# Hybrid encoder trunk on one core: attention steps queued ahead of waiting steps, the delta net's end cut into three steps, a residual's root ahead of a product

## The chip, the cores and the metric

The kernel runs on one core of a Trainium2 chip. TensorE (PE) multiplies matrices, VectorE (DVE), ScalarE (ACT) and GpSimd (POOL) do the rest, SyncE (SP) issues most of the transfers. Each engine works through its own queue in order, and semaphores tie the queues together. The metric is device time in microseconds (us), the median of several executions.

## The reference

Two layers over 256 tokens of width 2048. Each layer has a token mixer of three head groups on one input projection, and then a dense SwiGLU block; each of the two ends in a normed residual.

```python
def hybrid_layer(x, ...):
    h = rmsnorm(x, pre_mix_norm)
    proj = h @ w_in
    c_q, c_kv, conv_in, g_q, g_k, g_v, g_z, a_f, b_f, a_b, b_b = jnp.split(proj, ...)
    o_a = mla_mixer(c_q, c_kv, ...)          # attention, 8 heads
    o_b = conformer_conv(conv_in, ...)       # depthwise convolution, width 31
    o_c = gdn_mixer(g_q, g_k, g_v, g_z, ...) # delta net, 4 heads, both directions
    mix = jnp.concatenate([o_a, o_b, o_c], axis=-1) @ w_out
    x = x + rmsnorm(mix, post_mix_norm)
    h = rmsnorm(x, pre_ffn_norm)
    f = (jax.nn.silu(h @ w_gate) * (h @ w_up)) @ w_down
    return x + rmsnorm(f, post_ffn_norm)
```

All is float32. The end of the delta net is `rmsnorm(o_f + o_b, out_norm) * silu(z)`.

## The kernel before

A float32 product is made of three products: each operand is split into a high half and a remainder (`hilo`, lines 328 and 329), and L353, L354 and L355 multiply high by high, remainder by high and high by remainder. `dense` takes the weights in units of two blocks of 128 rows: one transfer of 512 KB into `ws`, the split into `wh` (ACT, L328) and `wl` (DVE, L329), then twelve products of 128x512 on PE. There are five buffers each of `ws`, `wh` and `wl`, so the split may run up to five units ahead of the products.

After each unit, `dense` calls `bg.step(BUDGET)`. The object `bg` holds the background tasks in a list: generators that issue a few instructions and yield a cost. A step takes tasks from the front of the list and lets each advance once, until the costs have used up the budget of 1.6. A negative yield sends a task to sleep for as many units. `add(..., first=True)` puts a task in front of the list, otherwise it goes to the end. `ensure(name)` runs a task to its end at once, with no product of `dense` in between.

The tasks of a mixer are, in short: `gdn` (the delta net: `gdn_prep`, then `gdn_mats` for four heads, then four `gdn_head` that advance together, then the end, L892 to L918), `att0` to `att3` (`attend`, two attention heads each) and `conf` (the convolution; it alone may advance more than once in a unit). What `gdn` does in order:

- In `gdn_mats` each head ends in two sums, the second of which is L736 on DVE; after the fourth head the 16x16 blocks go to DRAM and come back in another layout (tiles `cd` and `Mt`), and DVE inverts them row by row (L753, L755).
- `gdn_head` doubles the inverses in three levels (PE L795, L802, L806; DVE L797, L808, L810) and applies them in five stages, each one set of products on PE and then work on DVE or ACT: L819 and L821, L826 and L827 (ACT), L832, L833 and L837, L840 (ACT), L846 and L849, L857 and L860. Four heads follow one another in every stage.
- The end squares and sums the outputs (ACT L898, DVE L899), forms a reciprocal root of 8 columns in fourteen dependent small operations on DVE, scales twice (L909, L910) and transposes on PE (L914).

`attend` rotates the queries on DVE (`rotate`, L538 to L541, then the remainder L999), transposes the rotated half on PE (L1012), forms the scores (L1022 to L1026), the softmax (DVE L1028 to L1039, ACT L1033), transposes it (L1044) and multiplies by the values (L1051).

The mixer's output projection runs in two passes over the four blocks of columns: pass one takes the eight blocks of rows that belong to attention, pass two starts with the four of the delta net. Ahead of the first products of pass two stands `ensure("gdn")`. In the last block of columns of a residual's product, `ev` squares the result on ACT (L1204), weighs it on DVE (L1205), and calls `residual`, which forms the reciprocal root (L257 to L270) and adds to `xs` (L495).

The order in which instructions are written is changed once more when the program is put together: a scheduler lays each engine's queue out, so that the queue's order, not the text's, tells what stands ahead of what.

Of the kernel before, what the change touches and what calls it, by code (L numbers as in the profile page):

```python
# [13 lines left out]
ALU = mybir.AluOpType  # L14
# [39 lines left out]
def kernel(  # L54
# [8 lines left out]
    act, dve, pe, pool, sync = nc.scalar, nc.vector, nc.tensor, nc.gpsimd, nc.sync  # L63
# [9 lines left out]
    def U(dt=F32):  # L73
        return upool.tile([P, 512], dt, tag="u", name="u")

    def TP(dt=F32):
        return psb.tile([P, 512], dt, tag="tp", name="tp")

    def SM(n, tag=None):
        return small.tile([P, n], F32, tag=tag or f"sm{n}", name="sm")  # L80

    def v3(ap, a):
        return ap.rearrange("p (a b) -> p a b", a=a)
# [16 lines left out]
    first = const.tile([P, P], F32, name="first")  # L100
# [8 lines left out]
    ps = TP()  # L109
# [126 lines left out]
    def rsqrt(v, mul, eps, n, tag):  # L236

        w = SM(n, f"rsw{n}")
        y = SM(n, tag + "y")
        t = SM(n, f"rst{n}")  # L240
        dve.tensor_scalar(out=w, in0=v, scalar1=mul, scalar2=eps, op0=ALU.mult, op1=ALU.add)
        dve.tensor_scalar(out=y.bitcast(I32), in0=w.bitcast(I32), scalar1=1, scalar2=None,
                          op0=ALU.logical_shift_right)
        dve.tensor_scalar(out=y.bitcast(I32), in0=y.bitcast(I32), scalar1=-1,
                          scalar2=0x5F3759DF, op0=ALU.mult, op1=ALU.add)
        for _ in range(3):
            dve.tensor_tensor(out=t, in0=y, in1=y, op=ALU.mult)
            dve.scalar_tensor_tensor(out=t, in0=t, scalar=-0.5, in1=w, op0=ALU.mult, op1=ALU.mult)
            dve.scalar_tensor_tensor(out=y, in0=t, scalar=1.5, in1=y, op0=ALU.add, op1=ALU.mult)
        return y  # L250

    def rsqrt_sum(v, part, mul, eps, tag):

        pre = SM(1, tag + "p")
        dve.tensor_reduce(out=pre, in_=v, axis=AX.X, op=ALU.add)  # L257
        dve.tensor_scalar(out=pre, in0=pre, scalar1=eps / mul, scalar2=None, op0=ALU.add)
        w = SM(3, tag + "w")
        z = SM(1, tag + "z")  # L260
        a = SM(1, tag + "a")
        dve.tensor_scalar(out=w[:, 0:1], in0=part, scalar1=pre[:, 0:1], scalar2=64.0 * mul,
                          op0=ALU.add, op1=ALU.mult)
        dve.tensor_scalar(out=z.bitcast(I32), in0=w[:, 0:1].bitcast(I32), scalar1=-0.5,
                          scalar2=float(0x5F3759DF - 2 ** 31), op0=ALU.mult, op1=ALU.add)
        for i in range(1, 3):
            dve.tensor_scalar(out=w[:, i:i + 1], in0=w[:, 0:1], scalar1=4.0 ** -i, scalar2=None, op0=ALU.mult)
        for i in range(3):
            dve.scalar_tensor_tensor(out=a, in0=z, scalar=w[:, i:i + 1], in1=z, op0=ALU.mult, op1=ALU.mult)
            dve.scalar_tensor_tensor(out=z, in0=a, scalar=-3.0, in1=z, op0=ALU.add, op1=ALU.mult)  # L270
        return z
# [48 lines left out]
    bg = Background()  # L320
# [166 lines left out]
            dve.tensor_reduce(out=ssq[:, t:t + 1], in_=part, axis=AX.X, op=ALU.add)  # L487
        return rsqrt(ssq, 1.0 / DM, EPS, NT, name)

    def residual(t, parts, ssqp, rname):  # L490

        r = rsqrt_sum(ssqp[t][:, 0:3], ssqp[t][:, 3:4], 1.0 / DM, EPS, rname)
        for c in range(4):
            xv = xs[:, t, c * 512:(c + 1) * 512]
            ins = dve.scalar_tensor_tensor(out=xv, in0=parts[(c, t)], scalar=r[:, 0:1], in1=xv,  # L495
                                           op0=ALU.mult, op1=ALU.add)
        if t == 0:
            hold[:] = [(1, ins)]
# [9 lines left out]
    for l in range(DEPTH):  # L508
# [357 lines left out]
        def together(*gens):  # L866

            live = list(gens)
            while live:
                cost = rest = 0.0  # L870
                for g in list(live):
                    try:
                        c = next(g) or 0.0
                        rest = max(rest, -c)
                        cost += max(c, 0.0)
                    except StopIteration:
                        live.remove(g)
                yield -rest if rest > 0 else cost

        def gdn():  # L880
            bg.ensure("sq", "sk", "sv")
            while not G:
                yield -1
            yield from gdn_prep()
            yield from gdn_mats()
            if PAIRS:
                yield from together(gdn_head(0), gdn_head(1))
                yield from together(gdn_head(2), gdn_head(3))
            else:
                yield from together(*[gdn_head(h) for h in range(GH)])  # L890

            while not gz:  # L892
                yield -1
            rq = G["rn"][:, 0:8]
            ossq = SM(8, "ossq")
            for t in range(NT):
                sq = U()
                act.activation(out=sq, in_=osb[t], func=AF.Square)  # L898
                dve.tensor_reduce(out=ossq[:, t * 4:t * 4 + 4], in_=v3(sq, 4), axis=AX.X, op=ALU.add)  # L899
                yield 0.7  # L900
            rq2 = SM(8, "rq2")
            dve.tensor_tensor(out=rq2, in0=rq, in1=rq, op=ALU.mult)
            dve.tensor_tensor(out=ossq, in0=ossq, in1=rq2, op=ALU.mult)
            ro = rsqrt(ossq, 1.0 / (128.0 * 128.0), EPS, 8, "ro")
            dve.tensor_scalar(out=rq2, in0=rq, scalar1=128.0 ** -0.5, scalar2=None, op0=ALU.mult)
            dve.tensor_tensor(out=ro, in0=ro, in1=rq2, op=ALU.mult)
            yield 1.2
            for t in range(NT):
                dve.tensor_tensor(out=v3(osb[t], 4), in0=v3(osb[t], 4), in1=bc(ro[:, t * 4:t * 4 + 4], 2, P), op=ALU.mult)  # L909
                dve.tensor_tensor(out=osb[t], in0=osb[t], in1=gz[t], op=ALU.mult)  # L910
                yield 1.3
                ps = TP()
                for h in range(GH):
                    pe.transpose(ps[:, h * P:(h + 1) * P], osb[t][:, h * P:(h + 1) * P], ident)  # L914
                hi, lo = U(F32R), U(F32R)
                hilo_col(hi, lo, ps, vcol(l, ONORM, 0))
                ocT.append((hi, lo))
                yield 0.7  # L918


        obT = []
# [206 lines left out]
        def pair(hp):  # L1128
            qn = [U(), U()]
            kv = [U(), U()]  # L1130

            def ev_q(t, ps):
                act.activation(out=qn[t][:, 0:384], in_=ps, func=AF.Identity, scale=lq["r"][:, t:t + 1])

            def ev_kv(t, ps):
                act.activation(out=kv[t], in_=ps, func=AF.Identity, scale=lkv["r"][:, t:t + 1])
            bg.ensure("lq")
            dense(pair_lhs(lq["T"]), list(range(4)), 384, wload(w_uq[l], 384 * hp, 384), ev_q)
            bg.ensure("lkv")
            dense(pair_lhs(lkv["T"]), list(range(4)), 512, wload(w_ukv[l], 512 * hp, 512), ev_kv)  # L1140
            bg.ensure("rope_k")
            bg.add(f"att{hp}", attend(hp, qn, kv))

        for n, step in enumerate(ORDER.split()):
            kw = dict(pre=lambda: rxb.append(row_rstd(l, "rx")), head=HEADG, mid=mid_mix) if n == 0 else {}
# [14 lines left out]
            elif step == "ckv":  # L1160
                o, ssq = latent_kv()
# [15 lines left out]
        wpm = post_weight(post_mix_norm, l)  # L1177
# [8 lines left out]
        def out_proj(lhs, passes, w, wpm, rname, need, after0):  # L1186
            parts = {}
            ssqp = [SM(4, "ssqp0"), SM(4, "ssqp1")]
            for i, ks in enumerate(passes):
                last = i == len(passes) - 1  # L1190
                for nb in range(4):
                    if i == 0:
                        parts[(nb, 0)], parts[(nb, 1)] = U(), U()

                    def ev(t, ps):
                        o = parts[(nb, t)]
                        if not last:
                            act.copy(out=o, in_=ps)
                            return
                        if i > 0:  # L1200
                            dve.tensor_tensor(out=o, in0=o, in1=ps, op=ALU.add)
                            ps = o
                        junk = U()
                        act.activation(out=junk, in_=ps, func=AF.Square, accum_out=ssqp[t][:, nb:nb + 1])  # L1204
                        dve.tensor_tensor(out=o, in0=ps, in1=wpm[nb], op=ALU.mult)  # L1205
                        if nb == 3:
                            residual(t, parts, ssqp, rname)
                    dense(lhs, ks, 512, wload(w, nb * 512, 512), ev, need=need,
                          **(dict(tail=TAILG, after0=after0) if last and nb == 3 else {}))

# [250 lines left out]
```

## Time and profile before

| | |
|---|---|
| median of 3 runs | 2233.1 us (2231.53 to 2233.45) |
| the profiled execution | 2234.73 us, of which the span of the core's instructions is 2233.0 us |
| PE busy | 2203.0 us, 99% of the span, mean granted clock 0.998 |
| DVE busy | 1762.0 us, 79% of the span |
| ACT busy | 1182.5 us, 53% of the span |

"Busy" is the time in which an instruction of the engine was under way. PE is at work nearly all the time, so the time can change by the microseconds in which PE waits, or runs at half its clock. The granted clock is the share of 2.4 GHz that PE was given: 1.00 is 2.4 GHz, 0.50 would be 1.2 GHz.

### The profile page before, as it was taken

The page shows a single profiled execution, that of the slowest core. Times are in us where ns is not written, and L with a number is a line of the kernel's source. Part 1 is how long each engine was busy: PE and PEld are TensorE (multiplying, and loading weights), DVE is VectorE, ACT ScalarE, POOL GpSimd, SP SyncE. Part 2 cuts the span into 40 slices and gives each one's busy share as a digit, 9 for nine tenths or more (in the row PEclk, how much of TensorE's full clock was granted, in tenths as well). Part 3 has the DMA queues.
Part 4 walks back from the last instruction along what each step waited for, and adds up shares of the span by engine and source line. Part 5 has one row for each costly group of instructions (what it writes and reads, how often), then busy time and mean ns, then how long its engine had stood idle before and what let it go on. Part 6 is the DMA issues. An engine that isn't in the chain of part 4 may idle for free.

```text
span 2233.0 us, 29215 instructions
## 1 busy us (share of the span) xinstructions
PE 2203.0 (99%) x10483; PEld 1839.3 (82%) x10483; DVE 1762.0 (79%) x2873; ACT 1182.5 (53%) x1642; POOL 45.9 (2%) x93
## 2 busy tenths in 40 slices
PE   8999999999999999999999999999999999999998
PEld 7988887788888888888879888877888888888886
DVE  6777998899999897544486779979999998975444
ACT  6665545555555555444356655455555555554432
POOL 2000000000000000000000000000000000000000
PEclk9999999999999999999999999999999999999999
DMA  7554525546656656555556545245565566665553
GB/s 254 171 178 146 188 89 162 162 164 207 217 181 217 225 189 223 171 195 192 179 172 186 183 142 171 97 153 161 188 207 208 191 215 214 202 214 178 191 196 124
DMA packets 218545, 407.75 MB, mean 183 GB/s; under 512 B 17607, under 2 KB 30065, under 8 KB 218400
## 3 DMA queue, kind: packets, MB, share of 16 engines
q1 hardware_dynamic: 215360, 397.72, 54.3%
q0 software_dynamic: 3008, 8.16, 1.3%
q8 instruction: 82, 1.34, 0.2%
q14 instruction: 63, 0.52, 0.1%
q10 hardware_dynamic: 32, 0.01, 0.0%
HBM read 402.94 MB, written 2.90 MB: 182 GB/s over the span
## 4 chain that ended last, share of the span: by engine, by line
PE 92%; DVE 5%; DMA 1%; issue 0%; ACT 0%; SPq 0%; DVEq 0%; ACTq 0%; POOLq 0%
PE acc L1306 19%; PE tp L1306 19%; PE acc L353 16%; PE acc L354 16%; PE acc L355 16%; DVE wl L329 1%; DVE xs L495 1%; PE tp L1230 1%; PE tp L1051 1%; DVE u L950 1%; DMA cd<-u 1%; PE tp L795 0%; PE tp L802 0%; PE tp L1022 0%; DMA xs<-in_x_dram 0%
## 5 line engine op out<-in xcount | busy, mean ns | idle before, releaser
L328 ACT CAST wh<-ws 128x1024 fp32r<-128x1024 f32 (+3 forms) x820 | 815.5, 1010 | 795.2 <-PE acc L354 409.6
L329 DVE TENSOR_TENSOR wl<-ws,wh 128x1024 fp32r<-128x1024 f32 (+3 forms) x820 | 942.1, 1170 | 336.2 <-ACT wh L328 332.2
L353 PE MATMUL acc<-wh,u 128*128 128x512 f32 (+2 forms) x1792 | 695.5, 389 | 0.4
L354 PE MATMUL acc<-wh,u 128*128 128x512 f32 (+2 forms) x1792 | 686.2, 383 | 3.5 <-DVE u L329 1.8
L355 PE MATMUL acc<-wl,u 128*128 128x512 f32 (+2 forms) x1792 | 685.6, 383 | 3.0 <-DVE wl L329 3.0
L354 PEld LDWEIGHTS acc<-wh,u 128*128 128x128 f32 x1792 | 337.5, 188 | 68.4 <-DVE u L333 4.1
L355 PEld LDWEIGHTS acc<-wl,u 128*128 128x128 f32 x1792 | 336.8, 188 | 68.1 <-DVE wl L329 5.8
L353 PEld LDWEIGHTS acc<-wh,u 128*128 128x128 f32 x1792 | 337.3, 188 | 62.3 <-ACT u L332 2.5
L1306 PE MATMUL acc<-wh,u 128*128 128x512 f32 x1220 | 376.4, 389 | 0.0
L1306 PE MATMUL tp<-wh,u 128*128 128x512 f32 x1220 | 375.8, 389 | 0.0
L1306 PEld LDWEIGHTS acc<-wh,u 128*128 128x128 f32 x1220 | 228.7, 188 | 47.9 <-DVE u L329 0.6
L1306 PEld LDWEIGHTS tp<-wh,u 128*128 128x128 f32 x1220 | 228.9, 188 | 47.6
L1306 PE MATMUL acc<-wl,u 128*128 128x512 f32 x610 | 237.4, 389 | 0.0
L1306 PE MATMUL tp<-wl,u 128*128 128x512 f32 x610 | 237.3, 389 | 0.0
L1306 PEld LDWEIGHTS acc<-wl,u 128*128 128x128 f32 x610 | 114.5, 188 | 23.7
L1306 PEld LDWEIGHTS tp<-wl,u 128*128 128x128 f32 x610 | 114.5, 188 | 23.7
L950 DVE SCALAR_TENSOR_TENSOR u<-u,cols 128x241 f32<-128x241 f32 (+14 forms) x240 | 101.0, 470 | 0.0
L1344 ACT CAST wh<-ws 128x1024 fp32r<-128x1024 f32 x60 | 63.0, 1050 | 28.4 <-PE tp L1306 12.8
L1345 DVE TENSOR_TENSOR wl<-ws,wh 128x512 fp32r<-128x512 f32 x60 | 41.1, 686 | 23.8 <-ACT wh L1344 21.8
L328 ACT CAST u<-u 128x512 fp32r<-128x512 f32 (+2 forms) x48 | 27.8, 587 | 38.2 <-DVE u L448 34.2
L1329 ACT ACTIVATE u<-u,sm 128x512 f32<-128x512 f32 x40 | 28.8, 724 | 34.6 <-DVE u L1376 24.4
L1351 DVE TENSOR_TENSOR ws<-ws 128x512 f32<-128x512 f32 x60 | 41.5, 692 | 2.0
(303 smaller groups left out, 1541.8 us busy)
## 6 DMA issues: line engine op xcount, KB each, us to landing
ws<-in_w_gate_dram SPq DMA_DIRECT2D x176, 512.0 KB, 5.0
ws<-in_w_up_dram SPq DMA_DIRECT2D x176, 512.0 KB, 4.8
ws<-in_w_down_dram SPq DMA_DIRECT2D x176, 512.0 KB, 3.6
ws<-in_w_in_dram SPq DMA_DIRECT2D x112, 512.0 KB, 4.3
ws<-in_w_out_dram SPq DMA_DIRECT2D x64, 512.0 KB, 3.7
ws<-in_w_ukv_dram SPq DMA_DIRECT2D x16, 512.0 KB, 3.7
ws<-in_w_uq_dram SPq DMA_DIRECT2D x16, 384.0 KB, 3.5
ws<-in_w_in_dram SPq DMA_DIRECT2D x10, 444.0 KB, 4.1
```

Of the source, the lines that this page charges most:

```text
L328: act.copy(out=hi, in_=src)
L329: dve.tensor_tensor(out=lo, in0=src, in1=hi.bitcast(F32), op=ALU.subtract)
L353: pe.matmul(o, xh, rh, start=(i == 0), stop=False)
L354: pe.matmul(o, xl, rh, start=False, stop=False)
L355: pe.matmul(o, xh, rl, start=False, stop=(i == len(ks) - 1))
L495: ins = dve.scalar_tensor_tensor(out=xv, in0=parts[(c, t)], scalar=r[:, 0:1], in1=xv, op0=ALU.mult, op1=ALU.add)
L950: dve.scalar_tensor_tensor(out=o, in0=i, scalar=wc, in1=o, op0=ALU.mult, op1=ALU.add)
L1306: pe.matmul(o, a, b, start=count[i] == 1, stop=count[i] == total[i])
L1329: act.activation(out=sg[t], in_=x, func=AF.Silu, scale=rfb[0][:, t:t + 1])
L1344: act.copy(out=wh, in_=wg)
L1345: dve.tensor_tensor(out=wl[:, 0:512], in0=b11, in1=wh[:, 0:512].bitcast(F32), op=ALU.subtract)
L1351: dve.tensor_tensor(out=b21, in0=b21, in1=b22, op=ALU.subtract)
```

## The change

Three edits. Attention tasks are put in front of the list of background tasks instead of at its end. The end of the delta net yields three times (2.6, 2.0, 2.0) where it yielded seven times (0.7, 0.7, 1.2, 1.3, 0.7, 1.3, 0.7). In the last block of columns of a residual's product the weighing is written after the reciprocal root, not ahead of it. No instruction is added or taken away on PE, DVE, POOL or SP.

```diff
-    def residual(t, parts, ssqp, rname):
+    def residual(t, parts, ssqp, rname, weigh):
         r = rsqrt_sum(ssqp[t][:, 0:3], ssqp[t][:, 3:4], 1.0 / DM, EPS, rname)
+        weigh()
         for c in range(4):
...
                 dve.tensor_reduce(out=ossq[:, t * 4:t * 4 + 4], in_=v3(sq, 4), axis=AX.X, op=ALU.add)
-                yield 0.7
...
             dve.tensor_tensor(out=ro, in0=ro, in1=rq2, op=ALU.mult)
-            yield 1.2
+            yield 2.6
             for t in range(NT):
...
                 dve.tensor_tensor(out=osb[t], in0=osb[t], in1=gz[t], op=ALU.mult)
-                yield 1.3
                 ps = TP()
...
                 ocT.append((hi, lo))
-                yield 0.7
+                yield 2.0
...
             bg.ensure("rope_k")
-            bg.add(f"att{hp}", attend(hp, qn, kv))
+            bg.add(f"att{hp}", attend(hp, qn, kv), first=True)
...
-                        dve.tensor_tensor(out=o, in0=ps, in1=wpm[nb], op=ALU.mult)
+
+                        def weigh():
+                            dve.tensor_tensor(out=o, in0=ps, in1=wpm[nb], op=ALU.mult)
                         if nb == 3:
-                            residual(t, parts, ssqp, rname)
+                            residual(t, parts, ssqp, rname, weigh)
+                        else:
+                            weigh()
```

The change moves work along the queues at three places. Line numbers of the changed kernel differ by one or two from those before; the prediction uses the numbers of before.

**PE, the last stages of the delta net's heads.** Before, as queued, with products of `dense` (L353 to L355) between the stages:

```order
L826 MATMUL tp<-u 128x128 x8
L353 MATMUL acc<-wh,u 128x512
L354 MATMUL acc<-wh,u 128x512
L355 MATMUL acc<-wl,u 128x512
...
L832 MATMUL tp<-u 128x128
L833 MATMUL tp<-u 128x128
...
L846 MATMUL tp<-u 128x128 x8
...
L857 MATMUL tp<-u 128x128 x16
...
L914 MATMUL tp<-ident,u 128x128 x8
```

Between L826 and L832 stand twelve products of `dense`, as many between L833 and L846 and between L846 and L857, and 72 between L857 and the transposes L914. In the change the same stages (each line number one higher, L914 now L913) stand so:

```order
L827 MATMUL tp<-u 128x128 x8
L833 MATMUL tp<-u 128x128
L834 MATMUL tp<-u 128x128
...
L847 MATMUL tp<-u 128x128 x8
L858 MATMUL tp<-u 128x128 x16
L913 MATMUL tp<-ident,u 128x128 x8
L353 MATMUL acc<-wh,u 128x512
L956 MATMUL tp<-ident,u 128x128 x2
L354 MATMUL acc<-wh,u 128x512
```

What moved: the heads advance later, so that `ensure("gdn")` finds their last stages and the whole end still to do, and issues them in one piece; between L827 and L913 no product of `dense` is left.

**DVE, around the wait for the 16x16 blocks.** Before, the remainder of the rotated queries of the second attention task (L999) stands ahead of the first instruction that reads the blocks (L753):

```order
L736 TENSOR_REDUCE u<-tp 128x32
L329 TENSOR_TENSOR wl<-ws,wh 128x1024
L329 TENSOR_TENSOR u<-tp,u 128x256 x2
L538 TENSOR_TENSOR u<-u,tab 128x128
...
L329 TENSOR_TENSOR wl<-ws,wh 128x768
L999 TENSOR_TENSOR u<-u 128x4x64
L753 TENSOR_TENSOR u<-u 128x1
```

In the change the last sum over a head (now L737) comes after both evacuations of the convolution's gated input (L1124, before L1125), and the rotation for the third attention task (L539 to L542, L998) comes behind the first eight rows of the inversion (L754, L756):

```order
L1124 SCALAR_TENSOR_TENSOR u<-acc,sm,u 128x512 x2
L737 TENSOR_REDUCE u<-tp 128x32
L329 TENSOR_TENSOR wl<-ws,wh 128x768 x2
L946 TENSOR_SCALAR u<-u,cols 128x256 x4
L949 SCALAR_TENSOR_TENSOR u<-u,cols 128x241 x4
L949 SCALAR_TENSOR_TENSOR u<-u,cols 128x242 x2
L754 TENSOR_TENSOR u<-u 128x1
...
L539 TENSOR_TENSOR u<-u,tab 128x128
...
L329 TENSOR_TENSOR wl<-ws,wh 128x1024
L998 TENSOR_TENSOR u<-u 128x4x64
```

From L754 up to and with L998 there stand eight rows of the inversion (sixteen instructions), four of the convolution (L949), four splits of weights, eight instructions of the rotation and L998.

**DVE, the last residual of the program.** Before, the weighing (L1205) stands ahead of the root:

```order
L1205 TENSOR_TENSOR u<-acc,u 128x512
L262 TENSOR_SCALAR sm<-sm 128x1
L264 TENSOR_SCALAR sm<-sm 128x1
L267 TENSOR_SCALAR sm<-sm 128x1 x2
L269 SCALAR_TENSOR_TENSOR sm<-sm 128x1
```

In the change it stands behind the root's first instruction:

```order
L262 TENSOR_SCALAR sm<-sm 128x1
L1206 TENSOR_TENSOR u<-acc,u 128x512
L264 TENSOR_SCALAR sm<-sm 128x1
L267 TENSOR_SCALAR sm<-sm 128x1 x2
L269 SCALAR_TENSOR_TENSOR sm<-sm 128x1
```

The pair has changed places; what follows has not.

## Rows read from the trace of the kernel before

**Rows 1.** The page, part 1: busy us, share, instructions.
```profile
PE 2203.0 (99%) x10483; PEld 1839.3 (82%) x10483; DVE 1762.0 (79%) x2873; ACT 1182.5 (53%) x1642; POOL 45.9 (2%) x93
```

**Rows 2.** Waits of PE, both layers: us in total, times, longest.
```profile
PE tp L1044 <- DVE u L1039: 3.5, 6, 1.3
...
PE tp L914 <- DVE u L910: 3.2, 2, 1.6
```

**Rows 3.** Busy us in stretches: PE, PEld, DVE, ACT, POOL; then PEclk.
```profile
350.00:360.00 10.00, 8.38 (x44) 6.50 (x43) 10.00 (x38) 4.34 (x6) 0.00 (x0) 1.00 0.39 134
...
305.00:310.00 5.00, 4.89 (x17) 3.96 (x18) 3.91 (x9) 1.81 (x4) 0.00 (x0) 0.66 0.31 105
1412.00:1417.00 5.00, 4.36 (x22) 3.31 (x23) 4.95 (x14) 3.06 (x7) 0.00 (x0) 1.00 0.21 67
```

**Rows 4.** Timeline of PE, first layer: start, us, instruction, idle before.
```profile
304.13 0.72 PE L1044 MATMUL tp<-ident,u 128*128 128x128 f32 x4 [1.28 <-DVE u L1039]
```

**Rows 5.** Timeline of PE, end of the delta net, first layer.
```profile
330.72 3.73 PE L857 MATMUL tp<-u 128*128 128x128 f32 x32
...
350.18 0.39 PE L354 MATMUL acc<-wh,u 128*128 128x512 f32 x1
350.40 0.39 PE L355 MATMUL acc<-wl,u 128*128 128x512 f32 x1
352.41 1.26 PE L914 MATMUL tp<-ident,u 128*128 128x128 f32 x8 [1.62 <-DVE u L910]
```

**Rows 6.** Timelines of DVE and ACT over the same stretch.
```profile
334.53 0.48 DVE L860 TENSOR_TENSOR u<-u,tp 128x128 f32<-128x128 f32 x2
...
334.85 0.63 ACT L898 ACTIVATE u<-u 128x512 f32<-128x512 f32 x1 [3.06 <-DVE u L860]
...
335.70 0.68 DVE L899 TENSOR_REDUCE sm<-u 128x4 f32<-128x512 f32 x1
...
338.13 1.23 DVE L329 TENSOR_TENSOR wl<-ws,wh 128x1024 fp32r<-128x1024 f32 x1 [0.22 <-ACT wh L328]
339.27 1.61 DVE L950 SCALAR_TENSOR_TENSOR u<-u,cols 128x243 f32<-128x243 f32 x4
...
348.61 0.17 DVE L247 TENSOR_TENSOR sm<-sm 128x8 f32<-128x8 f32 x1
348.81 0.17 DVE L248 SCALAR_TENSOR_TENSOR sm<-sm 128x8 f32<-128x8 f32 x1
...
350.47 1.29 DVE L909 TENSOR_TENSOR u<-u,sm 128x512 f32<-128x512 f32 x2
351.67 1.29 DVE L910 TENSOR_TENSOR u<-u 128x512 f32<-128x512 f32 x2
```

**Rows 7.** Timeline of DVE around the transfer of the 16x16 blocks, first layer.
```profile
198.43 0.42 DVE L736 TENSOR_REDUCE u<-tp 128x32 f32<-128x256 f32 x1 [0.25 <-PE tp L734]
...
200.91 0.28 DVE L538 TENSOR_TENSOR u<-u,tab 128x128 f32<-128x128 f32 x1
...
202.37 0.22 DVE L541 TENSOR_TENSOR u<-u 128x64 f32<-128x64 f32 x1
...
208.74 0.16 DVE L753 TENSOR_TENSOR u<-u 128x1 f32<-128x1 f32 x1 [3.85 <-DMA u<-cd]
...
222.22 1.41 DVE L1125 SCALAR_TENSOR_TENSOR u<-acc,sm,u 128x512 f32<-128x512 f32 x2
```

**Rows 8.** Timeline of PE in a product of 384 columns.
```profile
219.41 0.34 PE L353 MATMUL acc<-wh,u 128*128 128x384 f32 x1
219.58 0.33 PE L354 MATMUL acc<-wh,u 128*128 128x384 f32 x1
```

**Rows 9.** Timeline of DVE, residual between the layers.
```profile
1112.50 0.69 DVE L1205 TENSOR_TENSOR u<-acc,u 128x512 f32<-128x512 f32 x1 [4.07 <-ACT u L1204]
1113.11 0.21 DVE L262 TENSOR_SCALAR sm<-sm 128x1 f32<-128x1 f32 x1
1113.35 0.15 DVE L264 TENSOR_SCALAR sm<-sm 128x1 int32<-128x1 int32 x1
```

## Prediction

> **What bounds the kernel now.** I read the page first. PE is busy 99% of the span, with 2203.0 us against DVE's 1762.0 [rows 1], so no work that leaves another engine can shorten the run; only PE's idle time, or PE at a lower clock, moves the end. Then I read the waits of PE. The change can touch two of them: L1044, which waits for the softmax, 3.5 us in both layers together, and L914, the transposes at the end of the delta net, 3.2 us, so 1.6 per layer [rows 2]. Then I read stretches. While the delta net runs, DVE is as full as PE: 10.00 of 10 us [rows 3]. PE's waits are thus small because work for DVE is written far enough ahead, not because DVE is idle. Last I read timelines of the places that the order shows as moved.
>
> Prices: a product of 512 columns follows the one before after 0.22 us (350.18 to 350.40 [rows 5]), one of 384 columns after 0.17 [rows 8]. On DVE a split of weights takes 1.14 us (338.13 to 339.27), a dependent operation on eight columns 0.20 (348.61 to 348.81), one step of the convolution 0.40 (four in 1.61), a scaling of 512 columns 0.6 to 0.65 [rows 6]. Eight transposes took 1.26 us [rows 5]. I make the sum against the median, 2233.1. The profiled execution took 2234.73 (span 2233.0); its own forecast is 1.6 us higher than that for the median.
>
> **The end of the delta net.** Before, PE's last stage of the heads (L857) starts at 330.72 and the transposes L914 at 352.41, with 72 products between; all the same PE waited 1.62 us [rows 5]. In the change nothing stands between them. The chain from one to the other doesn't shrink: both the yields that are gone and the list's order decide only what PE does meanwhile. After PE ends L857 there are on DVE's queue: the last two sums L860 0.48; the two splits of weights that the order puts behind the third and the fourth head, 2 x 1.14 = 2.28; two reductions L899, 0.68 + 0.6 = 1.28; fourteen small operations, 14 x 0.20 = 2.8; two scalings L909, 1.2; the first L910, 0.65, which lets the transposes start [rows 6]. That is 8.7 us. If both splits ran while PE was still in L857, 6.4. I take 8.7, as DVE is full there and comes late rather than early. Less the 1.6 of before, that makes +7.1 per layer, with bounds of 4.8 and 7.1.
>
> The stages ahead (L819 to L857) also lose the products between them. I cost that at nothing: four heads follow one another, PE needs 3.73 us for L857 [rows 5], and a stage gives DVE eight operations of about 0.25 us (two sums L860 in 0.48 [rows 6]), some 2 us. If that cover is gone, what shows is one step of latency, under 1 us a stage.
>
> What is late next: the convolution's end stands behind the delta net's on the same queue. From the last transposes L957 to L974 PE has 24 products, 5.3 us. DVE needs a split, 1.14, four operations of 512 columns, 2.4, and fourteen small ones, 2.8, together 6.3. So +1.0 per layer, with bounds of 0 (the small operations of two rows of tokens overlap fully) and 2.
>
> **Attention in front.** Here the mechanism is a transfer. DVE ends L736 at 198.43 + 0.42 = 198.85, and its next instruction that reads the 16x16 blocks, L753, starts at 208.74 after a wait for that transfer: 9.9 us, of which DVE stood still for 3.85 [rows 7]. Before, the rotation for an attention task stands ahead of L753, so nothing that PE wants soon is behind it. In the change the rotation of the third task and its remainder L999 stand behind, and PE's L1012 needs them. Count from the end of the product that the two L1125 evacuate. DVE: a handoff 0.4; two L1125 1.4 (1.41 for two) and L736 0.4; the transfer 9.9 (two splits, ten steps of the convolution, some 6 us, stand in it); then 4 splits 4.6, 16 small operations 3.2, 4 steps 1.6, eight operations of rotation 1.7 (200.91 to 202.37 + 0.22), L999 about 0.4 [rows 6, 7]. Sum 23.6. PE has 24 products of 384 columns 4.1, eight transposes 1.3, 24 of 512 columns 5.3, 24 of 384 columns 4.1, eight transposes 1.3, nine products 2.0: 18.1 [rows 5, 8]. So PE waits 5.5 us per layer. The bounds are 0 (DVE stood still 3.85 in the wait before; a transfer that returns 5.5 us sooner leaves nothing) and 6.
>
> On the other side attention no longer queues behind the delta net, and the L1044 waits should go: 3.5 / 2 = 1.75 per layer [rows 2]. Bounds 0 and 1.75; I take all. Net +3.75 per layer.
>
> **The clock.** After the 1.28 us wait of L1044 [rows 4] the stretch 305 to 310 ran at a granted clock of 0.66 with PE busy throughout: 5 x 0.34 = 1.7 us lost. The same wait in the second layer was followed by 1.00, and the 1.62 us of L914 by 1.00 as well [rows 3, 5]. So 1.3 to 1.6 us of idling cost the full clock once in three. The change gives two idle stretches of 5.5 and 8.7 us per layer. I take a drop from 2.4 to 1.2 GHz after each, at the price of the one that is seen: 4 x 1.7 - 1.7 (the old one goes) = +5.1. Bounds: -1.7 (none drops) and 4 x 3.4 - 1.7 = +11.9 (each lasts twice as long).
>
> The Trainium skill, "TensorE: Matmul & The Clock Gate", section "Why this matters for your kernels", asks to keep gaps between bursts of matmuls short, since the clock goes back to half rate after a long one. [...]
>
> **The residual's root.** The chain to the root loses a place behind L1205, which took 0.61 us (1112.50 to 1113.11), and L1205 now fills part of the 0.24 between L262 and L264 [rows 9]. L495 needs both, so only that slot is gained: 0.1 for each of the residuals. In a mixer's second residual the order also brings the four additions to `xs` ahead of one split and one operation of 512 columns: 1.14 + 0.6 = 1.7 in each layer if PE waits for them. I take -1.5 in all, between -3.5 and +1.2 (the weighing shows twice).
>
> **Sum.** 2 x (7.1 + 1.0 + 3.75) = 23.7; + 5.1 - 1.5 = +27.3. 2233.1 + 27.3 = 2260.4, **2260**. With every bound low: 2 x (4.8 + 0 - 1.75) - 1.7 - 3.5 = +0.9; with every bound high: 2 x (7.1 + 2 + 6) + 11.9 + 1.2 = +43.3.
>
> **Rivals.**
> First, faster: the end of the delta net is covered after all. The old waits go and nothing comes: -3.5 - 1.7 - 1.5 = -6.7, 2226.4. For it speaks that the whole of DVE's work is the same. Against it: with no product between L857 and L914 nothing of PE can cover a chain of fourteen dependent operations. It decides at 6.7 / 2 = 3.35 us of new idling per layer, so at a wait of 5.0 at L914, under the 6.4 of the low bound.
>
> Second, the tail alone: the blocks come back sooner, or DVE has read ahead, and the attention wait isn't there. 2 x (7.1 + 1.0 - 1.75) = 12.7; the clock drops twice instead of once, + 1.7; - 1.5: +12.9, 2246. For it: 5.5 is the difference of two sums of about 20, and a unit's split that comes a little earlier halves it. Against: the transfer's 9.9 us is measured and on one queue with what PE needs.
>
> Third, the clock stays low for twice as long after each gap: +6.8 on the forecast, 2267. For it: the gaps are four to seven times those seen. Against: PE has dense products behind them.
>
> Fourth, the change doesn't do what it says to PE: gains and losses balance within 0.2%, 2233. DVE would have to be several us ahead at both places, and rows 3 show no room in which it could get there.
>
> **How the numbers follow.** Forecast (tail, attention and four drops) 0.50; tail alone 0.22; clock low for longer 0.12; covered tail, faster 0.08; balance 0.05; stalls beyond these 0.03. The range 2240 to 2274 leaves out the last three, some 0.16 with the edges; the bounds' end of +43.3 (2276) is just outside, as it needs all at once. A change of 0.2%, 4.5 us, is about what a measurement of this kernel can tell from none, so same is 2228.6 to 2237.6: 0.05; faster 0.08, slower 0.87.
>
> **What would show it.** In the changed kernel's waits PE should show L913 behind DVE's L910 with some 17 us in two waits, and L1011 behind L998 (or the split, L355, just ahead of it) with 10 to 12 us in two; L1044's waits should be gone; the granted clock should dip after each of the four. DVE should stand still at L754 for the blocks as before. In the residuals L496 should start no later against the last product than L495 did. The prediction is wrong if DVE reaches the last L861 with the splits done, if the transfer's return moves, or if another product waits for a split that has slid behind L754, since PE would then lose more, and elsewhere.

## The result, and the profile after

The changed kernel takes 2263.6 us (median of 4, 2260.9 to 2264.9) against 2232.6 us before: a ratio of 1.0134, 95% interval 1.0118 to 1.0150. The profiled execution took 2260.9 us, its span is 2259.1 us, 26.1 us more than before's; the rows below are of it. The medians lie further apart, by 31.0 us: of the four executions of the changed kernel the profiled one is the shortest and has the highest mean granted clock (0.992, the others 0.990, 0.990 and 0.991), and the profiled execution of before (2234.7 us) is longer than the four that its median is taken from. First the page's part 1 (busy us, share, instructions), which answers to [rows 1]:

```profile
PE 2210.4 (98%) x10483; PEld 1846.6 (82%) x10483; DVE 1761.3 (78%) x2873; ACT 1179.8 (52%) x1638; POOL 45.9 (2%) x93
```

DVE has the same work in a longer span. PE waits more and also runs slower: 7.4 us more busy time with the same instructions. Next PE's waits (us in total, times, longest), which answer to [rows 2]:

```profile
PE tp L913 <- DVE u L910: 16.7, 2, 8.4
...
PE tp L1011 <- DVE u L998: 3.7, 4, 1.8
PE acc L355 <- DVE wl L329: 3.4, 2, 1.7
PE acc L353 <- ACT u L328: 2.9, 2, 1.4
...
PE tp L973 <- DVE sm L248: 1.7, 2, 0.8
PE tp L973 <- DVE u L964: 1.2, 2, 0.6
...
PE tp L1043 <- DVE u L1038: 0.7, 2, 0.3
```

The wait at the end of the delta net has gone from 3.2 to 16.7 us. Three waits behind it are new (L973 twice, then the products of the convolution's output, which wait for ACT): 2.9 us in each layer. Attention's waits moved from L1043 (L1044 before, 3.5 us) to L1011. The timeline of PE in the first layer answers to [rows 5]:

```profile
346.98 3.74 PE L858 MATMUL tp<-u 128*128 128x128 f32 x32
...
359.07 1.97 PE L913 MATMUL tp<-ident,u 128*128 128x128 f32 x8 [8.36 <-DVE u L910]
...
374.72 0.41 PE L973 MATMUL tp<-ident,u 128*128 128x128 f32 x2 [0.84 <-DVE sm L248]
375.74 0.88 PE L973 MATMUL tp<-ident,u 128*128 128x128 f32 x6 [0.61 <-DVE u L964]
378.05 1.20 PE L353 MATMUL acc<-wh,u 128*128 128x512 f32 x4 [1.43 <-ACT u L328]
```

DVE's timeline over that wait, answering to [rows 6]:

```profile
350.33 1.22 DVE L329 TENSOR_TENSOR wl<-ws,wh 128x1024 fp32r<-128x1024 f32 x1
351.47 0.48 DVE L861 TENSOR_TENSOR u<-u,tp 128x128 f32<-128x128 f32 x2
351.87 1.22 DVE L329 TENSOR_TENSOR wl<-ws,wh 128x1024 fp32r<-128x1024 f32 x1
353.00 1.27 DVE L900 TENSOR_REDUCE sm<-u 128x4 f32<-128x512 f32 x2
354.30 0.17 DVE L903 TENSOR_TENSOR sm<-sm 128x8 f32<-128x8 f32 x1
...
357.12 1.29 DVE L909 TENSOR_TENSOR u<-u,sm 128x512 f32<-128x512 f32 x2
358.34 1.28 DVE L910 TENSOR_TENSOR u<-u 128x512 f32<-128x512 f32 x2
```

This is the chain as it was counted, item by item, both splits (L329) in it, the first of them begun 0.4 us before PE's last product ended. Last, stretches of 5 us with a fallen clock (the column before the last two; busy us of PE first):

```profile
355.00:360.00 5.00, 0.93 (x5) 0.93 (x6) 4.24 (x15) 0.00 (x0) 0.00 (x0) 0.59 0.26 89
360.00:365.00 5.00, 5.00 (x20) 3.96 (x20) 1.50 (x2) 1.49 (x3) 0.00 (x0) 0.72 0.01 3
415.00:420.00 5.00, 3.10 (x8) 2.23 (x8) 5.00 (x12) 0.98 (x2) 0.00 (x0) 0.74 0.24 61
...
1475.00:1480.00 5.00, 2.62 (x10) 2.12 (x11) 3.58 (x7) 1.30 (x2) 0.00 (x0) 0.50 0.04 14
1480.00:1485.00 5.00, 5.00 (x20) 4.09 (x19) 0.88 (x3) 1.12 (x2) 0.00 (x0) 0.77 0.02 3
1495.00:1500.00 5.00, 3.57 (x12) 2.75 (x11) 2.12 (x3) 3.18 (x6) 0.00 (x0) 0.60 0.38 129
1500.00:1505.00 5.00, 5.00 (x17) 3.95 (x17) 1.00 (x1) 1.05 (x1) 0.00 (x0) 0.72 0.00 0
1540.00:1545.00 5.00, 5.00 (x19) 3.93 (x18) 5.00 (x10) 0.62 (x1) 0.00 (x0) 0.66 0.88 279
```

Busy time times what is missing from 1.00 is what the clock cost: 4.2 us behind the two long waits, 2.8 behind the wait for ACT in the second layer (1495 to 1505), 2.5 in the residuals; with a stretch at 0.92 behind the one at 415 (0.4 us), 10.0 us in all, where before had 1.7. Not all of it lengthens the run: where PE waits for DVE anyway, a slower product only takes the place of a wait (the residual's edit, below).

### The profile page after: what moved, and what is told of

Same layout as the page of the kernel before. It is cut to its first block, busy times and chain, and to the rows that moved or that the text cites. A ratio compares the mean times of both kernels' runs of the same rounds, so it can differ in the third digit from the quotient of the medians.

```text
span 2259.1 us, 29198 instructions
## 1 busy us (share of the span) xinstructions
PE 2210.4 (98%) x10483; PEld 1846.6 (82%) x10483; DVE 1761.3 (78%) x2873; ACT 1179.8 (52%) x1638; POOL 45.9 (2%) x93
## 4 chain that ended last, share of the span: by engine, by line
PE 92%; DVE 5%; DMA 1%; issue 1%; ACT 1%; SPq 0%; DVEq 0%; ACTq 0%; POOLq 0%
PE tp L1309 18%; PE acc L1309 18%; PE acc L353 16%; PE acc L355 16%; PE acc L354 16%; DVE wl L329 1%; PE tp L1233 1%; PE tp L1050 1%; DVE xs L496 1%; DMA cd<-u 0%; PE tp L803 0%; PE tp L796 0%; DVE u L949 0%; PE tp L439 0%; DMA xs<-in_x_dram 0%
## 5 line engine op out<-in xcount | busy, mean ns | idle before, releaser
L328 ACT CAST wh<-ws 128x1024 fp32r<-128x1024 f32 (+3 forms) x820 | 816.6, 1010 | 813.4 <-PE acc L354 424.8
L329 DVE TENSOR_TENSOR wl<-ws,wh 128x1024 fp32r<-128x1024 f32 (+3 forms) x820 | 943.5, 1170 | 367.0 <-ACT wh L328 361.5
L353 PE MATMUL acc<-wh,u 128*128 128x512 f32 (+2 forms) x1792 | 698.4, 390 | 3.2 <-ACT u L328 2.9
L354 PE MATMUL acc<-wh,u 128*128 128x512 f32 (+2 forms) x1792 | 690.2, 385 | 2.6 <-DVE u L329 1.2
L355 PE MATMUL acc<-wl,u 128*128 128x512 f32 (+2 forms) x1792 | 688.3, 384 | 3.4 <-DVE wl L329 3.4
L355 PEld LDWEIGHTS acc<-wl,u 128*128 128x128 f32 x1792 | 338.8, 189 | 67.1 <-DVE wl L329 4.0
L353 PEld LDWEIGHTS acc<-wh,u 128*128 128x128 f32 x1792 | 339.8, 190 | 65.8 <-ACT u L328 3.6
L354 PEld LDWEIGHTS acc<-wh,u 128*128 128x128 f32 x1792 | 339.2, 189 | 66.5 <-DVE u L333 3.9
L949 DVE SCALAR_TENSOR_TENSOR u<-u,cols 128x241 f32<-128x241 f32 (+14 forms) x240 | 100.6, 471 | 0.0
L328 ACT CAST u<-u 128x512 fp32r<-128x512 f32 (+2 forms) x48 | 27.9, 588 | 37.1 <-DVE u L448 32.8
```

The lines of the kernel that those rows point to most:

```text
L328: act.copy(out=hi, in_=src)
L329: dve.tensor_tensor(out=lo, in0=src, in1=hi.bitcast(F32), op=ALU.subtract)
L353: pe.matmul(o, xh, rh, start=(i == 0), stop=False)
L354: pe.matmul(o, xl, rh, start=False, stop=False)
L355: pe.matmul(o, xh, rl, start=False, stop=(i == len(ks) - 1))
L949: dve.scalar_tensor_tensor(out=o, in0=i, scalar=wc, in1=o, op0=ALU.mult, op1=ALU.add)
```

## The experiments

**One part at a time.** The diffs are the three pieces of the change, each alone on the kernel before.

The residual's edit:

> Only the residual's edit. Theory (the end of the delta net carries the change): nothing moves in the mixer, the two waits of L914 stay at about 1.6 us each, and the five residuals give back about 0.2 us each, so some 1 us less than before, 2231.5. Rival (the residual's edit costs by itself, since the weighing moves behind the root): 0.6 us for each of five residuals, 2235.6.

Measured: 2232.9 against 2233.7, ratio 0.9997 (0.9989 to 1.0006): no change to be measured. In the first layer's residual PE's longest wait is now 1.70 us (before it was 0.95), and the clock falls behind it, where before it was 1.00. A row of PE and the stretch behind it:

```profile
404.99 0.50 PE L355 MATMUL acc<-wl,u 128*128 128x512 f32 x1 [1.70 <-DVE wl L329]
```
```profile
405.00:410.00 5.00, 5.00 (x15) 3.96 (x16) 5.00 (x10) 0.62 (x1) 0.00 (x0) 0.66 0.70 211
```

The fallen clock costs nothing here: it takes the place of shorter waits for DVE (0.28, 0.27 and 0.17 us before) that would follow. PE's transposes L439 around this place in the first layer, from before (clock 1.00), from the three steps alone (below; 0.66) and from the residual's edit alone (0.66):

```profile
401.20 0.38 PE L439 MATMUL tp<-ident,xs 128*128 128x128 f32 x2
414.27 0.66 PE L439 MATMUL tp<-ident,xs 128*128 128x128 f32 x4 [0.17 <-DVE u L448]
```
```profile
401.65 0.38 PE L439 MATMUL tp<-ident,xs 128*128 128x128 f32 x2
413.28 2.09 PE L439 MATMUL tp<-ident,xs 128*128 128x128 f32 x16
```
```profile
400.06 0.38 PE L439 MATMUL tp<-ident,xs 128*128 128x128 f32 x2
412.57 0.60 PE L439 MATMUL tp<-ident,xs 128*128 128x128 f32 x4
```

From the start of the first row of each pair to the end of the second there are 13.7 us before, 13.7 with three steps and a fallen clock, and 13.1 with the residual's edit and a fallen clock. So the edit gains 0.6 us at this place, too little for the median to tell. Over all profiles the clock falls behind this wait in 13 of 14 layers with the edit (1.70 us) and in 5 of 12 without it (0.95 us); that the longer wait makes it fall is likely, not shown.

Attention in front:

> Only the attention tasks in front; the end of the delta net keeps its seven steps. Theory: the delta net is late at the second pass, and the call that finishes it runs all its steps in one piece whatever their number, so PE waits 8.4 us at L914 in each layer, as in the full change, and the time is that of the full change plus the 1 us of the residuals: 2264 to 2266. Rival (the three long steps carry the loss): PE waits clearly less than 8.4 us, and the time is under 2245.

Measured: ratio 1.0120 (1.0105 to 1.0136). The trace comes from a second run of the same kernel.

> The kernel with attention in front alone once more, for its trace. Theory: PE waits 8.4 us at L914 in each layer as in the full change, though the end has seven steps; 2262. Rival: clearly shorter waits, with more of the loss elsewhere.

Measured: ratio 1.0113 (1.0094 to 1.0131), and the same wait as in the full change, to 0.01 us:

```profile
358.34 1.97 PE L914 MATMUL tp<-ident,u 128*128 128x128 f32 x8 [8.36 <-DVE u L910]
```

So attention in front carries most of the loss, with seven steps in the end as with three. The waits at L974 (1.45 us a layer) and at the product behind it are there too. The time is a little below the 2264 to 2266 expected.

The three steps:

> Only the three steps. Theory: between L857 and the transposes there are 61 products where there were 72, 13.6 us, more than the chain of 8.5 us on DVE, so no new long wait; the time stays within 2 us of before, 2231 to 2235. Rival (the three steps push the transposes ahead of what they wait for): the 11 products that are gone turn into waiting, 11 x 0.22 = 2.4 us per layer, 2237.5.

Measured: 2237.5, ratio 1.0016 (1.0007 to 1.0024). The time is the rival's, the mechanism neither: no wait at the transposes is left, but the three waits behind it are there as in the full change, and the clock falls after them (0.66 from 365 to 370):

```profile
362.38 0.41 PE L972 MATMUL tp<-ident,u 128*128 128x128 f32 x2 [0.84 <-DVE sm L248]
363.39 0.88 PE L972 MATMUL tp<-ident,u 128*128 128x128 f32 x6 [0.61 <-DVE u L963]
365.70 1.65 PE L353 MATMUL acc<-wh,u 128*128 128x512 f32 x3 [1.43 <-ACT u L328]
```

Here the end of the delta net is done earlier and the convolution's end stands by itself, its products right behind its last transposes. Before, the two ends stood side by side, with products of `dense` among them.

**Half of the attention tasks.**

```diff
-            bg.add(f"att{hp}", attend(hp, qn, kv))
+            bg.add(f"att{hp}", attend(hp, qn, kv), first=hp < 2)
```

> Only the first two attention tasks of each layer in front, the other two at the end as before; seven steps, old residual. Between L857 and the transposes there are 24 products (5.3 us) where there were 72 before and none in the change. Theory (DVE's chain of about 8.4 us less what PE has to do meanwhile): PE waits some 3.1 us at the transposes, plus up to 2.9 us at L974 and the product behind it as in the full change, while the two waits of L1044 (1.5 us each) go: about 2233 + 2 x (3.1 - 1.6 + 2.9 - 1.7) = 2238, and up to 2 us more for the clock. Rival (that attention stands in front costs by itself, by DVE's order at the 16x16 blocks): more than half of the loss stays, 2248 or more.

Measured: 2295.3, ratio 1.0272 (1.0258 to 1.0286): the theory is wrong by far. The rival's "2248 or more" holds, and the loss does come from DVE's order at the 16x16 blocks, but through a task that is not in front. Two rows of PE and one of DVE, first layer:

```profile
259.38 0.72 PE L1012 MATMUL tp<-identr,u 128*128 128x128 f32 x4 [17.77 <-DVE u L999]
...
374.82 1.54 PE L914 MATMUL tp<-ident,u 128*128 128x128 f32 x6 [7.56 <-DVE u L910]
```
```profile
230.50 0.16 DVE L753 TENSOR_TENSOR u<-u 128x1 f32<-128x1 f32 x1 [2.64 <-DMA u<-cd]
...
258.82 0.41 DVE L999 TENSOR_TENSOR u<-u 128x256 fp32r<-128x256 f32 x1
```

The wait that was forecast for attention is here at 17.8 us: the third task's rotation, no longer in front, stands behind all fifteen rows of the inversion and the steps of the convolution between them, and those behind the transfer. And 24 products between L857 and L914 took only 0.8 us off the wait at L914: two splits of weights stand on DVE between the last L860 and L910, and each of them waits for a product (`L329 <- ACT L328 <- PE L354`). Cover from products lengthens the chain it is to cover.

**The chain at the end of the delta net.**

```diff
-    def rsqrt(v, mul, eps, n, tag):
+    def rsqrt(v, mul, eps, n, tag, steps=3):
...
-        for _ in range(3):
+        for _ in range(steps):
...
-            ro = rsqrt(ossq, 1.0 / (128.0 * 128.0), EPS, 8, "ro")
+            ro = rsqrt(ossq, 1.0 / (128.0 * 128.0), EPS, 8, "ro", steps=6)
```

> The changed kernel with six steps of the iteration for the reciprocal root at the delta net's end where it has three: nine more small operations on DVE in the chain between L857 and the transposes, in each layer. Theory (PE waits for exactly this chain): nine operations at 0.20 us, 1.8 us, are added to each of the two waits of L913, 8.4 becomes 10.2, and the time grows by 3.6 us, to about 2267. Rival (PE waits for something else that ends about then, a transfer or a split of weights): the waits stay at 8.4 and the time within 1 us of the changed kernel's.

Measured: ratio 1.0150 against the full change's 1.0134, 0.0016 x 2233 = 3.6 us. The wait:

```profile
PE tp L913 <- DVE u L910: 20.3, 2, 10.2
```

The intervals of the two ratios overlap, so the waits decide, and they are 3.6 us longer, as forecast: PE waits for this chain, operation by operation.

**The clock.**

```diff
+            ps = TP()
+            for i in range(34):
+                pe.matmul(ps[:, 0:P], ident, ident, start=True, stop=True)
             rq = G["rn"][:, 0:8]
```

> The changed kernel with 34 products of 128x128 (an identity by itself, which nothing reads) between L857 and the transposes, at about 0.23 us each 7.9 us in each layer, less than the 8.4 us for which PE stands still there. The wait for DVE stays, PE is at work in it. Theory (the stand-still also costs the clock: after it the granted clock was 0.59 and 0.72 over ten us in the first layer, 0.71, 0.50 and 0.77 in the second): the clock stays at 1.00 behind the transposes and 2 to 2.5 us per layer come back, so 4 to 5 us, about 2259. Rival (the clock is no part of the loss): the time stays within 1.5 us of the changed kernel's, and the fallen clock is only where nothing waits for PE.

Measured: ratio 1.0097 (1.0083 to 1.0111), 8.3 us below the full change (0.0037 x 2233), more than expected. The stretch behind the filled gap in each layer:

```profile
355.00:360.00 5.00, 4.23 (x37) 3.86 (x36) 4.15 (x14) 0.36 (x1) 0.00 (x0) 1.00 0.26 94
...
1475.00:1480.00 5.00, 4.51 (x25) 3.65 (x26) 3.92 (x11) 1.29 (x2) 0.00 (x0) 1.00 0.01 3
```

With PE at work in the gap the clock stays at 2.4 GHz. Not all of the 8.3 us is the clock's: the order puts four of L957's eight transposes and two of L974's earlier, and the waits at L974 shrink from 1.45 to 0.5 us a layer. From the first transposes (L913) to the residual's first L439 the changed kernel takes 51.75 us in the first layer and 55.08 in the second, the kernel with the filled gap 49.23 and 49.22: 8.4 us less, of which 1.95 are those waits. The other 6.4 are the clock's, where the rows of the changed kernel gave 7.1 for the transposes and the wait for ACT.

**Everything earlier.** `BUDGET = 2.0` in the changed kernel.

> The changed kernel with a budget of 2.0 a unit where it has 1.6, so that the background steps run earlier: 60 products lie between L857 and the transposes where there were 72 before and none in the change. Theory (the loss is that the delta net is late, not that attention stands in front): no wait above 1.6 us at the transposes, and L1043 doesn't wait long either; 2230 to 2238. Rival (attention in front costs by itself): 2250 or more. Either may be off where DVE's queue lets another instruction stand behind a wait.

Measured: 2248.5, ratio 1.0070 (1.0057 to 1.0082), between the two. The wait at the transposes is down to 2.4 us, but others have come. PE's waits, and DVE in the first layer:

```profile
PE tp L913 <- DVE u L910: 4.9, 2, 2.4
PE tp L931 <- DVE u L1124: 4.6, 4, 2.0
```
```profile
221.99 0.16 DVE L754 TENSOR_TENSOR u<-u 128x1 f32<-128x1 f32 x1 [4.53 <-DMA u<-cd]
...
224.08 0.74 DVE L1124 SCALAR_TENSOR_TENSOR u<-acc,sm,u 128x512 f32<-128x512 f32 x1
```

DVE stands still for the 16x16 blocks, now with L1124 behind them, and PE's transposes L931 wait for L1124. This is the mechanism of the attention term once more, with another victim.

**Is there a better order?** Three runs put the third and fourth attention task right behind the delta net, ahead of the convolution, so that the delta net isn't delayed:

```diff
+                if first == "gdn" and "gdn" in rest:
+                    for k in list(rest):
+                        self.tasks[k] = rest.pop(k)
+                        if k == "gdn":
+                            break
...
-            bg.add(f"att{hp}", attend(hp, qn, kv))
+            bg.add(f"att{hp}", attend(hp, qn, kv), first="gdn" if hp > 1 else False)
```

With the residual's edit:

> The kernel before with the residual's edit, and with the third and fourth attention tasks put right behind the delta net in the list, ahead of the convolution: the delta net is not delayed. 72 products between L857 and the first transposes, then 24 from L957 to L974 and the convolution's products right behind, as in the run with three steps alone. Theory: the waits of L1044 go (3.0 us and a clock drop of 1.7), those of L914 too (3.2), but the convolution's end, with three splits of weights in its chain, makes PE wait 2.9 us per layer and drops the clock, 2 x 2.9 + 2.4; with 0.8 from the residuals, 2233. Rival (only a delayed delta net costs anything): 2225 to 2227.

Measured: 2233.9, ratio 1.0004 (0.9995 to 1.0013). L1044 and L914 wait no more; L974 (here L980) and the product behind it wait 2.9 us a layer, as the theory had it.

With a step of the convolution at a cost of 0.3 (was 0.7), without and with the residual's edit:

> The kernel before with the third and fourth attention tasks right behind the delta net in the list, and with the cost of a step of the convolution set to 0.3 where it was 0.7, so that more of them are taken in a unit. The order has the softmax of the last task far ahead of the call that needs it, and the end of both the delta net and the convolution as before (72 products, then the transposes L914 and L957 side by side, one split less in the convolution's chain). Theory (it is lateness at the calls that finish a task that costs, each with its clock drop): the waits of L1044 go, 3.0 us of idling and 1.7 us of clock, and nothing comes in their place; 2228 to 2230. Rival (DVE is full there, and what is taken early makes something else late): 2233 or more.

> The same with the residual's edit. Theory (the edit gathers several short waits of PE into one of 1.7 us, after which the granted clock falls, 1.7 us; it saves 2.4 us of idling in the first layer and pays 1.7): within 1 us of the run without it. Rival (the edit is a gain where the rest of the kernel doesn't hide it): 2 us or more below the run without it.

Measured: 2233.0, ratio 0.9997 (0.9988 to 1.0006), and 2233.7, ratio 0.9998 (0.9988 to 1.0007). The waits of L1044 went, and those of L914 (here L919) grew from 3.2 to 5.5 us, with a fallen clock (0.67) behind the first:

```profile
PE tp L919 <- DVE u L915: 5.5, 2, 2.7
```

So the rival held in its number; that it is DVE's fullness which brings the waits back is not shown. Three orders in which neither attention nor the delta net's heads are late all end within 1 us of before.

**Less work for DVE.** On the kernel with the early convolution, six of the 31 steps go to GpSimd:

```diff
+            side = order[-6:]
+            yside = [U(), U(), U(), U()]
+                    pool.tensor_scalar(out=m, in0=i, scalar1=wc, scalar2=None, op0=ALU.mult)
+                    pool.tensor_tensor(out=o, in0=o, in1=m, op=ALU.add)
...
-            for n, j in enumerate(order):
+            for n, j in enumerate(order[:-6]):
...
+            for c in range(2):
+                dve.tensor_tensor(out=yacc[c], in0=yacc[c], in1=yside[c], op=ALU.add)
```

> The kernel with the convolution early and two attention tasks behind the delta net, with six of the 31 steps of the convolution done on GpSimd beside DVE (a product and an addition each, 48 operations a layer, into sums of their own, which DVE adds at the end). From DVE this takes 24 x 0.40 = 9.6 us a layer and adds 1.3, between the attention tasks and the delta net's end. Theory (DVE is full in that stretch, so that waits of PE taken away at one place come back at another: 2233 in five arrangements): with 8.3 us a layer less for DVE the waits at the transposes, 2.7 us in each layer, and the one drop of the clock, 1.7 us, go: 2226 to 2228. Rival (the waits are the length of dependent chains and not the amount of DVE's work): they stay above 2 us and the time stays at 2232 to 2234. A second rival: operations of GpSimd and DVE hinder each other, DVE's steps show well over 0.40 us each, and the time is 2235 or more.

Measured: 2294.1, ratio 1.0272 (1.0258 to 1.0286). The theory and the first rival are wrong by far. The second rival's "2235 or more" holds, and DVE was slower while GpSimd worked (from 237.62 four steps in 2.30 us, else 1.6; from 239.84 a split of 1.74, else 1.2), but that is a few of 60 us. The rest is a wait that none of them had. Rows of PE, of ACT and of GpSimd, first layer:

```profile
275.96 0.45 PE L1066 MATMUL tp<-ident,u 128*128 128x128 f32 x1 [28.27 <-DVE u L1061]
```
```profile
273.96 0.47 ACT L1055 ACTIVATE u<-tp,sm 128x256 f32<-128x256 f32 x1 [29.19 <-POOL u L957]
```
```profile
273.24 1.34 POOL L957 TENSOR_TENSOR u<-u 128x241 f32<-128x241 f32 x2
```

The exponentials of the softmax wait for GpSimd's L957. They read nothing of it, so what they wait for is the buffer `u` into which they write: GpSimd's chain, begun at 235.7, gave it back with the first of these two additions, at about 273.9. The list of PE's waits holds no L914 and no L974 any more, which speaks for the theory, but DVE stood still for 28 us too. What the order would give with buffers of its own for `yside` was not tried.

## Why the prediction was right, and where its terms were not

The forecast was 2260 in 2240 to 2274, the time is 2263.6. By the medians the kernel lost 31.0 us where 27.3 were forecast; the profiled executions, which alone show the terms, lie 26.1 apart. Term by term, in profiled time, both layers together:

| term | forecast | measured |
|---|---|---|
| end of the delta net | +14.2 | 16.7 - 3.2 = +13.5 |
| what follows on it | +2.0 | L973 and L353: +5.8 |
| attention | +11.0 - 3.5 | L1011 +3.7, L1043 -2.8 |
| clock, without the residuals | +5.1 | 7.1 - 1.7 = +5.4 |
| residuals and the rest | -1.5 | 26.1 less the above, +0.5 |
| sum | +27.3 | +26.1 |

**The end of the delta net** was right in mechanism and size: 8.36 us where 8.7 stood, all of its items in the rows, and dosed by the run with nine operations more. That the stages ahead cost nothing was right too: PE has no wait between L820 and L858.

**What follows** was mis-sized: 2.9 us a layer, not 1.0. The chain to L973 had two splits in it (369.30 and 372.24), not one, 1.14 us more. And a link was missing: the products behind L973 are the convolution's own, and wait 1.43 us for ACT and DVE. The runs with three steps alone and with attention alone both have these waits: either edit brings them by itself.

**Attention** was the step that failed in size. The wait was forecast at 5.5 us and is 1.8 (with a second of 0.2). These rows answer to [rows 7]:

```profile
222.01 0.41 DVE L737 TENSOR_REDUCE u<-tp 128x32 f32<-128x256 f32 x1
...
231.47 0.16 DVE L754 TENSOR_TENSOR u<-u 128x1 f32<-128x1 f32 x1 [2.58 <-DMA u<-cd]
...
231.93 0.15 DVE L756 TENSOR_REDUCE u<-u 128x1 f32<-128x1 f32 x1
232.00 0.46 DVE L949 SCALAR_TENSOR_TENSOR u<-u,cols 128x242 f32<-128x242 f32 x1
...
240.46 0.42 DVE L998 TENSOR_TENSOR u<-u 128x256 fp32r<-128x256 f32 x1
```

From L754 to the end of L998 there are 9.4 us, not 11.5: a small operation that stands between independent ones adds 0.07 us (231.93 to 232.00) to 0.17 (the larger ones), 1.6 us for all sixteen, not the 0.20 each of a dependent row. The transfer took 231.47 - 222.42 = 9.05, not 9.9. About 1 us more lies ahead of it: L737 ended 1.2 us after PE's first product of 384 columns began (221.27), where the sum had 2.2 for the handoff, L1125 and L736. As a difference of two sums of about 20, the term lost two thirds to an error of some 15% in one. The mechanism stands, as the runs with half of the tasks (17.8 us) and with the larger budget show.

**The clock** was right in size, in part by luck. Four drops were forecast, two behind each of the two kinds of wait. There were two behind the transposes (4.24 us), none behind L1011, and one behind L353 (2.83), which wasn't on the list. Two more in the residuals, 2.9 us by the rows, stand in the last line of the table, since a fallen clock adds nothing there.

**The residual's edit** was forecast to gain 1.5, most of it from the mixer's second residual. The root itself got shorter by what was counted: in the last residual of the program from 2.38 us (2224.69, L1205, to 2227.07, L495) to 2.26 (2250.90, L262, to 2253.16, L496). In the mixer's second residual the gain is 0.6 us, not up to 1.7. In the median it can't be told from nothing, nor from 1.5.

So the sum is right in part by luck: attention's 6.6 us too much stands against 3.8 too little in what follows and 2.0 in the residuals and the rest.

## What to carry to other kernels

When a call finishes a background task in one piece, find what its chain of dependent operations is on the other engine; with no products left between, the engine that bounds the kernel waits out all of it, and it costs more by the clock. Count a small operation at the step of a dependent row (0.20 us here) only where such a row stands alone; between independent operations it added 0.07 to 0.17. And where the second engine is full too (DVE was busy for 69.4 of 70 us from 230 to 300 us before), a new order can move waits about: here three orders with the late piece repaired all came out where the old one was.

## What was not expected of the hardware

The granted clock fell after waits that differ little in length. At the residual's L355 it fell behind 1.70 us in 13 of 14 layers, and behind 0.95 us in 5 of 12 (both layers with the three steps alone, neither before). It fell after 1.28 us once of two before, and not after 1.62 us (L914, twice). At L1011 it did not fall after 1.77 us in the changed kernel; with the gap filled it fell there after 1.85 us in the first layer (0.66 from 240 to 245) and not after 2.35 us in the second. The length of the last wait alone doesn't say it, and what does was not found.

On GpSimd one product of some 241 to 246 columns by a scalar for each partition took 0.90 us in the median and one addition 0.69, where DVE does both in one step of 0.40. While DVE was at work too, products of 246 columns took 1.31 us in the mean.
